# One store of a tree-masked attention kernel issued as two DMAs, of 60 and of 68 partitions

## The chip, the cores and the metric

The kernel runs on one core of one Trainium2 chip. The metric is the device time of one execution in microseconds (us). The inputs and outputs lie in the chip's memory (HBM), and the time includes loading the inputs and storing the result.

## The reference

Attention over 8 x 12 = 96 heads of 512 positions and 64 dimensions, in fp32. The mask is a binary tree: position i may look at itself and at its ancestors, (i-1)//2 and so on up to 0.

```
for i in range(seq):
    mask[i, i] = 1
    parent = i
    while parent > 0:
        parent = (parent - 1) // 2
        mask[i, parent] = 1
scores = einsum('bhqd,bhkd->bhqk', Q, K) * scale + (1 - mask) * (-1e9)
weights = softmax(scores)            # with the row's maximum taken off
out = einsum('bhqk,bhkd->bhqd', weights, V)
```

## The kernel before

A head's 512 rows lie on 128 partitions, four rows to a partition: a partition holds 4 x 64 fp32 values of one head, 1 KB in a row, both in HBM and in the output tile.

The 96 heads are worked in 48 pairs (`NP`), two heads at a time. Four heads are a quad (`NQ` = 24), and one output tile `of` holds a quad, so it is filled by two pairs: quad q by the pairs 2q and 2q + 1. There are 22 such tiles (`NOUT`), so that quads 22 and 23 take the tiles of quads 0 and 1 again.

The main loop (L644) goes over the pairs. For each it computes the scores on TensorE with the mask added as a code product, takes the exponent on ScalarE, multiplies by V and by a column of ones on TensorE (`values`), and divides on VectorE (`norm`, L495 and L496: a reciprocal and a product that writes `of`). Work on pair i - 1's values stands in the loop's step i. The order of the steps is written out by hand, and so are the queues.

GpSimd issues nearly all loads and stores. Its list (`pool_program`) has 21 stores of a whole quad (512 KB each, `store`, L503 and L504) in a fixed order with the loads and some copies; the last of them is that of quad 21. Five pieces of the output are not in this list:

- Quad 19 is stored by SyncE in the loop's step 41 (`store_apart`, L514 to L520), as two DMAs: the partitions 0 to 59 and 60 to 127 (`APART_ROWS` = 60).
- The pairs 44, 45 and 46 are stored by SyncE one at a time, in the loop's steps 45, 46 and 47 (L677 and L678), each by one DMA of 128 partitions and two heads, 256 KB. The heads of a pair are two apart in its quad.
- Of pair 47, SyncE stores one head and ScalarE the other (L680 and L681), 128 KB each.

A store waits for the product of `norm` that fills its part of `of`. SyncE has nothing else to do after the first loads: its instructions are issued in the order above, each when its wait is over. At the end the program waits until all stores have landed.

Of the kernel before, what the change touches and what calls it, by code (L numbers as in the profile page):

```python
# [98 lines left out]
def kernel(  # L99
# [7 lines left out]
    nc = tc.nc  # L107
    B, H, S, D = Q.shape
    P = nc.NUM_PARTITIONS
# [18 lines left out]
    Or = out.rearrange("b h (p t) d -> p (b h) (t d)", t=4)  # L128
# [71 lines left out]
    qTs, kTs, kqps, obs, ets, ofs = {}, {}, {}, {}, {}, {}  # L200
# [151 lines left out]
    def evac(i):  # L352
        if i >= WIDE:
            return evac_wide(i)
        kq = work.tile([P, 2, 16, 32], bf16, name="kq")
        kTs[i] = kq[:, 0, :, :]
        qTs[i] = kq[:, 1, :, :].rearrange("p (t u) c -> p t (u c)", t=4)
        src = kqps[i][:, :, 0:18, :]
        src = bass.AP(
            src.tensor, src.offset,  # L360
            [list(src.ap[0]), [1024, 2], [32, 8], [9 * 32, 2], [1, 32]],
        )
        nc.vector.tensor_copy(  # L363
            out=kq[:, :, :, :].rearrange("p k (x y) c -> p k x y c", y=2), in_=src
        )
# [4 lines left out]
    def scores1(i):  # L370

        sp = psS.tile([P, 2, 512], fp32, name="s1")
        for a in range(2):
            nc.tensor.matmul(  # L374
                out=sp[:, a, :], lhsT=k1code[64 * a:64 * a + CODE_ROWS, :],
                rhs=(q1code[64 * a:64 * a + CODE_ROWS, :] if i < WIDE
                     else q1wide[64 * a:64 * a + CODE_ROWS, :, :]),
                start=True, stop=False,
            )
        for a in range(2):  # L380
            nc.tensor.matmul(  # L381
                out=sp[:, a, :], lhsT=keys(i, a, TOP),
                rhs=qTs[i][64 * a:64 * a + 64, :, :].rearrange("p t c -> p (t c)"),
                start=False, stop=True,
            )
        et = etpool.tile([P, 2, 4, 128], bf16, name="e1")
        nc.scalar.activation(
            out=et[:, :, :, :].rearrange("p a t c -> p (a t c)"),
            in_=sp[:, :, :].rearrange("p a c -> p (a c)"),
            func=AF.Exp, scale=scale,  # L390
        ) if i < WIDE else nc.scalar.activation(  # L391
            out=et[:, :, :, :].rearrange("p a t (r u) -> p a (t r) u", u=2),
            in_=sp[:, :, :].rearrange("p a (u c) -> p a c u", u=2),
            func=AF.Exp, scale=scale,
        )
        ets[i] = et
# [31 lines left out]
    def scores2(i):  # L428
        if i >= WIDE:
            return scores2_wide(i)  # L430
        sp = psS.tile([P, 2, 4, 128], fp32, name="s2")
        flat = sp[:, :, :, :].rearrange("p a t c -> p a (t c)")
        for a in range(2):
            nc.tensor.matmul(
                out=sp[:, a, :, 32:128], lhsT=k2code[64 * a:64 * a + CODE_ROWS, :],
                rhs=q2code[64 * a:64 * a + CODE_ROWS, :].rearrange(
                    "p (t c) -> p t c", t=4
                )[:, :, 32:128],
                start=True, stop=False,
            )  # L440
        for t, lo, hi in ((2, 32, 192), (0, 192, 256), (3, 288, 448), (1, 448, 512)):
            for a in range(2):
                nc.tensor.matmul(
                    out=flat[:, a, lo:hi], lhsT=keys(i, a, TILE2[t]),
                    rhs=qTs[i][64 * a:64 * a + 64, :, :].rearrange("p t c -> p (t c)")[:, lo:hi],
                    start=False, stop=t == 1, skip_group_check=t in (2, 3),
                )
        nc.scalar.activation(
            out=e2s[i % NE][:, :, :, 32:128].rearrange("p a t c -> p (a t) c"),
            in_=sp[:, :, :, 32:128].rearrange("p a t c -> p (a t) c"),  # L450
            func=AF.Exp, scale=scale,
        )

    def values(i):

        if i < NP - 1:
            obs[i] = ob = psO.tile([P, 2, 512], fp32, name="ob")
        else:
            obs[i] = ob = psS.tile([P, 2, 512], fp32, name="s1")
        e1, e2, vt = ets[i], e2s[i % NE], vts[(head(i, 0) // VB) % NV]  # L460

        assert all(("vt", n, head(i, a)) in issued for n in range(10) for a in range(2))

        def product(e, a, t, tile_v, lo=0, hi=128, **flags):
            nc.tensor.matmul(  # L465
                out=ob[lo:hi, a, 65 * t:65 * t + 65],
                lhsT=e[:, a, PLACE[t], lo:hi],
                rhs=vt[:, head(i, a) % VB, tile_v, 0:D + 1],
                **flags,
            )  # L470

        def halves(a):
            for t in (0, 1):
                product(e2, a, t, 1 + SELF[t], 0, 64, start=False, stop=t == 1)
                product(e2, a, t, 1 + t, 64, 128, start=False, stop=t == 1)

        for a in range(2):
            for t in range(4):
                product(e1, a, t, 0, start=t == 0, stop=False)
            for t in (2, 3):  # L480
                product(e2, a, t, 1 + t, start=False, stop=False)
            if i == NP - 1:
                halves(a)
        if i < NP - 1:
            for a in range(2):
                halves(a)

    def norm(i):
        q, r = divmod(i, 2)
        if r == 0:  # L490
            ofs[q] = opool.tile([P, 4, 4, D], fp32, name="of")
        o4 = obs[i][:, :, 0:260].rearrange("p a (t c) -> p a t c", c=D + 1)
        rec = small.tile([P, 2, 4, 1], fp32, name="rec")
        for a, n in ((0, 2),) if i < NP - 1 else ((0, 1), (1, 1)):
            nc.vector.reciprocal(out=rec[:, a:a + n, :, :], in_=o4[:, a:a + n, :, D:D + 1])  # L495
            nc.vector.tensor_tensor(  # L496
                out=ofs[q][:, head(i, a) % 4:head(i, a + n - 1) % 4 + 1:head(i, 1) - head(i, 0), :, :],
                in0=o4[:, a:a + n, :, 0:D],
                in1=rec[:, a:a + n, :, :].to_broadcast([P, n, 4, D]),
                op=ALU.mult,  # L500
            )

    def store(eng, q, h0=0, n=4, step=1):  # L503
        return eng.dma_start(  # L504
            out=Or[:, 4 * q + h0:4 * q + h0 + step * (n - 1) + 1:step, :],
            in_=ofs[q][:, h0:h0 + step * (n - 1) + 1:step, :, :].rearrange(
                "p h t d -> p h (t d)"
            ),
        )


    APART, APART_AT, APART_ROWS = 19, 41, 60

    def store_apart():  # L514

        for p0, p1 in ((0, APART_ROWS), (APART_ROWS, P)):
            nc.sync.dma_start(
                out=Or[p0:p1, 4 * APART:4 * APART + 4, :],
                in_=ofs[APART][p0:p1, :, :, :].rearrange("p h t d -> p h (t d)"),
            )  # L520
# [123 lines left out]
    for i in range(NP + 1):  # L644
        steps = FIRST[i] if i < len(FIRST) else "SVT" if done < SIDE else "SVKQ"
        for step in steps:
            if step == "S" and i < NP:
                scores1(i)
                scores2(i)
            if step == "V" and i >= 1:  # L650
                values(i - 1)
                norm(i - 1)
                valued = True
            if step == "T" and done < NP:
                transpose(done)
                evac(done)
                done += 1
            if step == "K" and done < NP:
                transpose(done, (0,))
            if step == "Q" and done < NP:  # L660
                transpose(done, (1,))
                evac(done)
                done += 1
            if step == "X":
                spin("s1" if valued else "ob", 2)
            if step == "D":
                spread_by(nc.vector.tensor_copy, BY_VECTOR, STEADY_VECTOR, i)
            if step == "A":
                spread_by(nc.scalar.copy, BY_SCALAR, STEADY_SCALAR, i)
        if "D" not in steps:  # L670
            spread_by(nc.vector.tensor_copy, BY_VECTOR, STEADY_VECTOR, i)
        if "A" not in steps:
            spread_by(nc.scalar.copy, BY_SCALAR, STEADY_SCALAR, i)
        pool(i)
        if i == APART_AT:
            store_apart()
        if i >= NP - 3 and i < NP:  # L677
            store(nc.sync, (i - 1) // 2, (i - 1) % 2, 2, 2)  # L678
    assert not program
    store(nc.sync, NQ - 1, 1, 1)  # L680
    store(nc.scalar, NQ - 1, 3, 1)  # L681
# [30 lines left out]
```

## Time and profile before

| | |
|---|---|
| median of 3 runs | 136.35 us (135.78 to 136.41) |
| profiled execution, its own time | 136.35 us |
| its span, first to last instruction | 134.5 us |
| mean granted TensorE clock | 0.982 |
| busy: PE, VectorE, ScalarE, GpSimd | 116.7, 105.3, 110.9, 82.5 us |
| moved by DMA | HBM read 37.92 MB, written 12.58 MB |

The span runs from the first to the last instruction of the core; the execution's own time has 1.85 us around it. The profile gives start and length of each instruction, and for DMAs the issue on the issuing engine (SPq, ACTq and POOL are the queues of SyncE, ScalarE and GpSimd), the packets of each queue and the time from issue to landing. The queue called q0 carries GpSimd's transfers, q1 SyncE's and q10 ScalarE's. A DMA is carried out by up to 16 DMA engines side by side, each of which adds one to the transfer's semaphore when its part has landed. The trace records these increments.

### The profile page before, as it was taken

What the parts mean: (1) busy time and instruction counts of PE and PEld (TensorE: products, weight loads), DVE (VectorE), ACT (ScalarE), POOL (GpSimd) and SP (SyncE); (2) the same over time, 40 slices, a digit from 0 to 9 for tenths busy, and PEclk for the clock granted to TensorE, in tenths of its full rate; (3) what the DMA queues carried; (4) which work ended last, traced back from release to release, by engine and by line L of the source; (5) the groups of instructions that cost most, each with busy time, mean ns of one, the idle gap of its engine ahead of it and who ended that gap; (6) DMA issues with size and microseconds to landing.
All of it is one profiled execution on the core that took longest, in us unless ns stands there. A gap on an engine that the chain in (4) does not pass through costs nothing.

```text
span 134.5 us, 5483 instructions
## 1 busy us (share of the span) xinstructions
PE 116.7 (87%) x2385; PEld 79.7 (59%) x2385; DVE 105.3 (78%) x231; ACT 110.9 (82%) x169; POOL 82.5 (61%) x111
## 2 busy tenths in 40 slices
PE   6876989998797997799999899989899999999900
PEld 2342765665575665567576576757657676776600
DVE  2328699878969999987989979999598899666530
ACT  4359989989999899999999997979997797787800
POOL 6988636647465969899922279742999459512000
PEclk9999999999999999999999999999999999999975
DMA  4999999999999999999999999999999999999981
GB/s 126 215 168 193 202 192 197 199 200 196 201 199 204 198 198 196 208 198 201 198 205 197 310 251 204 289 271 240 323 212 329 229 293 400 403 398 405 374 319 44
DMA packets 37516, 32.23 MB, mean 240 GB/s; under 512 B 1357, under 2 KB 34765, under 8 KB 37493
## 3 DMA queue, kind: packets, MB, share of 16 engines
q0 software_dynamic: 35120, 29.63, 118.5%
q1 hardware_dynamic: 1813, 1.81, 4.0%
q10 hardware_dynamic: 560, 0.46, 1.1%
q8 instruction: 18, 0.29, 0.8%
q14 instruction: 5, 0.04, 0.1%
HBM read 37.92 MB, written 12.58 MB: 375 GB/s over the span
## 4 chain that ended last, share of the span: by engine, by line
PE 33%; ACT 23%; DVE 16%; DMA 15%; issue 7%; POOL 2%; ACTq 0%; POOLq 0%
PE ob L465 11%; DMA kst<-in_K_dram 10%; ACT vt L271 8%; ACT e L422 8%; DVE vt L271 6%; DMA vst<-in_V_dram 5%; DVE of L496 5%; PE s L374 4%; PE kqp L289 4%; ACT e L391 4%; PE s L406 4%; PE s L381 3%; PE kqp L319 3%; PE s L416 3%; DVE kq L347 2%
## 5 line engine op out<-in xcount | busy, mean ns | idle before, releaser
L391 ACT ACTIVATE e<-s 128x1024 bf16<-128x1024 f32 x40 | 40.9, 1023 | 8.8 <-PE s L381 7.9
L465 PE MATMUL ob<-vt,e 128*128 128x65 bf16 (+1 forms) x940 | 37.1, 197 | 3.0 <-DVE of L496 2.3
L465 PEld LDWEIGHTS <-e 128*128 128x128 bf16 (+1 forms) x960 | 30.3, 102 | 10.7 <-DVE of L496 2.2
L422 ACT ACTIVATE e<-s 128x384 bf16<-128x384 f32 x80 | 34.7, 489 | 0.0
L496 DVE TENSOR_TENSOR of<-ob,rec 128x512 f32<-128x512 f32 x47 | 32.5, 691 | 1.6
L271 DVE COPY vt<-vst 32x1024 bf16<-32x1024 bf16 (+8 forms) x56 | 29.9, 534 | 2.5 <-DMA vst<-in_V_dram 1.0
L271 ACT COPY vt<-vst 32x512 bf16<-32x512 bf16 (+5 forms) x30 | 23.4, 779 | 1.2 <-DMA vst<-in_V_dram 0.6
L504 POOL DMA_DIRECT2D out_dram<-of x21 | 16.2, 773 | 10.7 <-DVE of L496 3.4
L208 POOL DMA_DIRECT2D kst<-in_K_dram x19 | 16.0, 843 | 9.1 <-PE ob L465 2.9
L271 POOL COPY vt<-vst 32x256 bf16<-32x256 bf16 (+1 forms) x28 | 19.4, 693 | 2.7 <-DMA vst<-in_V_dram 1.6
L374 PE MATMUL s<-codes 40*128 40x512 bf16 x96 | 19.1, 393 | 1.8 <-ACT e L391 1.0
L495 DVE RECIPROCAL rec<-ob 128x8 f32<-128x8 f32 x47 | 9.6, 205 | 13.1 <-PE ob L465 12.2
L208 POOL DMA_DIRECT2D vst<-in_V_dram x17 | 14.1, 835 | 8.0 <-DMA vst<-in_V_dram 3.9
L289 PE MATMUL kqp<-ptile,kst 128*64 128x128 bf16 x320 | 16.6, 223 | 2.3 <-DVE kq L363 1.2
L381 PE MATMUL s<-kq 64*128 64x512 bf16 x96 | 18.4, 377 | 0.0
L343 DVE COPY kq<-kqp 128x512 bf16<-128x512 bf16 x40 | 16.6, 415 | 0.1
L416 PEld LDWEIGHTS <-kq 64*128 64x128 bf16 x320 | 12.3, 94 | 4.7
L406 PE MATMUL s<-codes 40*128 40x384 bf16 x80 | 13.7, 334 | 1.3
L416 PE MATMUL s<-kq 64*128 64x160 bf16 (+1 forms) x320 | 14.7, 208 | 0.0
L289 PEld LDWEIGHTS <-kst 128*64 128x64 bf16 x320 | 11.5, 111 | 4.8 <-issue 2.9
L223 POOL DMA_DIRECT2D qst<-in_Q_dram x13 | 9.6, 740 | 6.7 <-DMA vst<-in_V_dram 3.7
L347 DVE COPY kq<-kqp 128x1024 bf16<-128x1024 bf16 x20 | 13.6, 681 | 0.0
(37 smaller groups left out, 102.3 us busy)
## 6 DMA issues: line engine op xcount, KB each, us to landing
out_dram<-of POOLq DMA_DIRECT2D x21, 512.0 KB, 12.3
vst<-in_V_dram POOLq DMA_DIRECT2D x9, 512.0 KB, 12.3
kst<-in_K_dram POOLq DMA_DIRECT2D x8, 512.0 KB, 14.0
qst<-in_Q_dram POOLq DMA_DIRECT2D x7, 512.0 KB, 12.6
qst<-in_Q_dram POOLq DMA_DIRECT2D x8, 256.0 KB, 9.4
vst<-in_V_dram POOLq DMA_DIRECT2D x4, 256.0 KB, 8.7
kst<-in_K_dram POOLq DMA_DIRECT2D x4, 256.0 KB, 9.7
kst<-in_K_dram POOLq DMA_DIRECT2D x7, 128.0 KB, 9.2
```

The source lines that it names most:

```text
L208: return nc.gpsimd.dma_start(out=kept[b][:, h0 % size:h0 % size + n, :, :].rearrange("p h t d -> p h (t d)"), in_=src[:, h0:h0 + n, :],)
L271: return copy(out=dst, in_=src)
L289: nc.tensor.transpose(out=dst, in_=src, identity=perm)
L343: nc.vector.tensor_copy(out=kTs[i].rearrange("p (x y) c -> p x y c", y=2), in_=src)
L374: nc.tensor.matmul(out=sp[:, a, :], lhsT=k1code[64 * a:64 * a + CODE_ROWS, :], rhs=(q1code[64 * a:64 * a + CODE_ROWS, :] if i < WIDE else ...
L381: nc.tensor.matmul(out=sp[:, a, :], lhsT=keys(i, a, TOP), rhs=qTs[i][64 * a:64 * a + 64, :, :].rearrange("p t c -> p (t c)"), start=False, ...
L391: ) if i < WIDE else nc.scalar.activation(
L406: nc.tensor.matmul(out=flat[:, a, :, :].rearrange("p u (t c) -> p u t c", t=4)[:, :, :, 16:64], lhsT=k2code[64 * a:64 * a + CODE_ROWS, :], ...
L416: nc.tensor.matmul(out=flat[:, a, :, lo:hi], lhsT=keys(i, a, TILE2[t]), rhs=qT[64 * a:64 * a + 64, :, lo:hi], start=False, stop=t == 1, sk ...
L422: nc.scalar.activation(out=e2s[i % NE][:, a, :, 32:128].rearrange("p t (r u) -> p t r u", u=2), in_=flat[:, a, :, :].rearrange("p u (t r) ...
L465: nc.tensor.matmul(out=ob[lo:hi, a, 65 * t:65 * t + 65], lhsT=e[:, a, PLACE[t], lo:hi], rhs=vt[:, head(i, a) % VB, tile_v, 0:D + 1], **flags,)
L496: nc.vector.tensor_tensor(out=ofs[q][:, head(i, a) % 4:head(i, a + n - 1) % 4 + 1:head(i, 1) - head(i, 0), :, :], in0=o4[:, a:a + n, :, 0: ...
```

## The change

Pair 44's store becomes two DMAs on SyncE, of the partitions 0 to 59 and 60 to 127, with the same two heads. The stores of the pairs 45 and 46 go through the new helper too, as one DMA of 128 partitions each, with the access patterns that they had. Nothing is moved in the order of any other engine; SyncE has one more instruction. In the new file the helper shifts the line numbers: its DMA is L516, `store_apart`'s L524.

```
     APART, APART_AT, APART_ROWS = 19, 41, 60
+
+    def store_rows(i, p0, p1):
+        q, h0 = divmod(i, 2)
+        return nc.sync.dma_start(
+            out=Or[p0:p1, 4 * q + h0:4 * q + h0 + 3:2, :],
+            in_=ofs[q][p0:p1, h0:h0 + 3:2, :, :].rearrange("p h t d -> p h (t d)"),
+        )
 
     def store_apart():
...
         if i >= NP - 3 and i < NP:
-            store(nc.sync, (i - 1) // 2, (i - 1) % 2, 2, 2)
+            for p0, p1 in ((0, APART_ROWS), (APART_ROWS, P)) if i - 1 in (44,) else ((0, P),):
+                store_rows(i - 1, p0, p1)
     assert not program
```

## The prediction

> **What bounds the kernel now.** I read the windows of the last 25 us first, then SyncE's timeline, the DMA page and SyncE's waits. The columns of the windows are the length, each engine's busy time, the granted clock, the DMA engines' mean busy share and GB/s.
>
> ```profile
> 115.00:120.00 5.00, 5.00 (x107) 3.49 (x103) 3.11 (x7) 4.03 (x8) 1.93 (x3) 1.00 1.04 401
> 120.00:125.00 5.00, 5.00 (x104) 3.40 (x97) 3.31 (x8) 3.92 (x8) 0.75 (x1) 1.00 1.03 401
> 125.00:129.50 4.50, 2.63 (x54) 1.77 (x50) 2.72 (x8) 2.20 (x5) 0.00 (x0) 1.00 0.96 358
> 129.50:132.00 2.50, 0.00 (x0) 0.00 (x0) 0.00 (x0) 0.00 (x0) 0.00 (x0) 0.51 0.68 238
> 132.00:134.50 2.50, 0.00 (x0) 0.00 (x0) 0.00 (x0) 0.00 (x0) 0.00 (x0) 0.50 0.05 17
> ```
>
> Compute is over before 129.5. What follows is transfers alone, and they do not end together: 238 GB/s, then 17 GB/s. A last stretch at 17 GB/s is a few of the 16 DMA engines finishing after the rest have gone idle. SyncE's own issues (start, length), and VectorE's last product:
>
> ```profile
> 112.43 0.35 SPq L517 DMA_DIRECT2D out_dram<-of  x1
> 123.64 0.40 SPq L504 DMA_DIRECT2D out_dram<-of  x1
> 125.76 0.39 SPq L504 DMA_DIRECT2D out_dram<-of  x1
> 127.73 0.37 SPq L504 DMA_DIRECT2D out_dram<-of  x1
> 128.48 1.13 SPq L504 DMA_DIRECT2D out_dram<-of  x1
> 128.58 0.42 DVE L496 TENSOR_TENSOR of<-s,rec 128x256 f32<-128x256 f32 x1
> ```
>
> The 123.64 row is pair 44's store, the one that is cut in two. Then come pairs 45 and 46 and one head of pair 47. The DMA page (queue: packets, MB, share; issues: KB each, us to landing), and from SyncE's waits the one at the end:
>
> ```profile
> q1 hardware_dynamic: 1813, 1.81, 4.0%
> ...
> out_dram<-of SPq DMA_DIRECT2D x3, 256.0 KB, 6.1
> ...
> out_dram<-of SPq DMA_DIRECT2D x1, 272.0 KB
> ...
> out_dram<-of SPq DMA_DIRECT2D x1, 240.0 KB, 8.5
> out_dram<-of SPq DMA_DIRECT2D x1, 128.0 KB, 4.7
> out_dram<-of ACTq DMA_DIRECT2D x1, 128.0 KB, 3.8
> ```
>
> ```profile
> SPq L707 <- DMA out_dram<-of: 3.4, 2, 2.8
> ```
>
> The last SyncE store lands at 128.48 + 4.7 = 133.2 us and ScalarE's at 129.03 + 3.8 = 132.8. SyncE waits for them, and the span closes 1.3 us after the last landing. So the end is set by one DMA engine.
>
> **Which engine, and why.** The 272 KB row has no landing time. Quad 19 is already stored in 60 and 68 partitions, and this is its 68-row part. The packet count says why. SyncE's queue carries 40 packets of codes, 256 of first K, 512 of quad 19, 3 x 256 of pairs 44 to 46 and 128 of the last head: 1704. The other 109 of the 1813 are 4-byte semaphore writes, one for each DMA engine that a transfer uses: five transfers on 128 partitions make 5 x 16 = 80, the codes' 40 rows make 10, the 60 rows 15, and so the 68 rows make 4. In short, 60 rows go over 15 engines, 68 rows over only four, 17 rows each.
>
> The trace's landing records agree. The semaphore of the 68-row part has four late increments, at 129.34, 129.85, 130.06 and 130.55 us. Pair 44's last increment is at 131.21, pair 45's at 131.89, pair 46's at 132.54, ScalarE's at 132.88, SyncE's last at 133.22. Each step is one engine's share: 16 KB in 0.65 to 0.68 us, and 16 KB for the two single heads together. Only an engine that still owed 68-row packets until 130.55 can be 0.66 us behind it with pair 44. So the engine that ends the kernel, call it X, is one of the four that carry quad 19's 17 rows. From 130.55 it moves 64 packets of 1 KB in 2.67 us, 41.8 ns each. The last increments of the final store fall into groups: nine engines by 131.15, three at 131.70 to 131.93, three at 132.52 to 132.73, X at 133.22. Nine engines thus have 2.07 us of slack, X has none.
>
> **The change, part by part.**
> Removed: one DMA of 128 partitions, 16 KB on each of 16 engines. Added: 60 partitions, 4 rows x 2 KB = 8 KB on each of 15 engines, and 68 partitions, 17 rows x 2 KB = 34 KB on each of four. Bytes in all are the same. If the four are quad 19's four, and the 15 contain them, each of the four goes from 16 to 42 KB. The 16th engine loses 16 KB, the others 8 KB.
>
> Cost on X: 26 more packets of 1 KB behind the same earlier work. X's rate while GpSimd's stores also run on it is a round of one 4 KB packet and one 1 KB packet in 0.203 us (the spacing of the last GpSimd packets), 25.2 bytes per ns, so 26.6 thousand bytes cost at least 1.06 us. Alone, X takes 41.8 ns a packet by the landings and 42.3 by the spacing of its last packets: 1.09 to 1.10 us. I take 1.09, since X's GpSimd packets must be done by the time pair 44 moves in 0.66 us. The added semaphore write on X is already in the 41.8 ns, which is averaged over packets and their semaphore writes.
>
> Cost on SyncE: one more issue, 0.35 us by the 112.43 row, 1.13 us by the longest row. It starts at about 124.04 and the next store is ready only at 125.76, so 1.72 us of waiting covers either end. Behind it on SyncE are only stores; if the cover were gone, they would start up to 0.4 us later, which is still not on the path, because X owes earlier packets throughout.
>
> Cost for compute: nothing. GpSimd's last store is issued at 121.4, before the change, and no later tile takes the buffers of quads 22 or 23. VectorE, ScalarE and TensorE wait for no store in the rows after 123.64, so VectorE should still end near 129.0.
>
> Gain elsewhere: eleven engines lose 8 KB and one of them 16 KB, 0.33 to 0.66 us. They already end before X, so this is worth nothing.
>
> Sum: X lands at 133.22 + 1.09 = 134.31, the span becomes 134.5 + 1.09 = 135.6, and the profiled execution's 136.35 becomes 137.44. Its time equals the median of the runs (135.78 to 136.41), so no shift is needed. +1.09 us is +0.8%.
>
> The Trainium skill ("DMA: Bandwidth & Descriptors", section "Why a DMA increments its semaphore by 16 and not by 1") says that the engine count is the largest number up to 16 that divides the slowest dimension, and that SyncE's transfers take the lowest-numbered engines. The counts 15, 4 and 10 agree; that the four are always the same ones is shown by no row here, and by that rule the sum stands as above.
>
> **The rivals.**
> *Another four engines (not slower).* If the engines of a narrow transfer are dealt out in turn, the 34 KB miss X. X then only loses 8 KB, 0.33 us, and ends at 132.89. An early engine goes to at most 131.15 + 1.09 = 132.24. The time is 136.35 - 0.33 = 136.0, or 137.0 if the four include the engine that ends at 132.73. It decides as soon as X is outside the second four. Against it: quad 19's parts are the only ones on four engines, so nothing shows a second choice either way. Chance 0.06.
>
> *No concentration.* The change does not do what I read from the counts: the halves share all engines, and the time stays 136.35. The 109 semaphore writes and the four late landings speak against it. Chance 0.04. The same page of the Trainium skill ("Rules for kernel authors") says that two transfers to disjoint halves both spray over all 16 engines and are just not worth it. By that the time would not move; the 272 KB row disagrees for 68 partitions.
>
> *SyncE stalls behind the backlog (slower still).* The last issue took 1.13 us where the others take 0.4, though nothing else ran on SyncE: it may have met a full queue. With 26 more packets pending, later issues may be held longer. As long as X still has packets, this costs nothing on X. It counts if SyncE is held until an earlier store has landed. A store needs about 1.55 us from issue to its first landing (ScalarE: 129.03 to 130.58), plus 0.33 us for its 8 KB. Held until pair 45 has landed on X (131.89 + 1.09 = 132.98), the last head would land at 134.86: 138.0 us. Held until pair 46 (133.63): 135.51, 138.6 us. The 123.64 and 125.76 rows, unheld with quad 19's backlog on X, speak against it. Chance 0.07.
>
> **How the numbers follow.** The forecast, the same four engines, has 0.83, and the time is its own: 137.4. Its own spread is the price's 1.06 to 1.10 plus the runs' 0.6 us, 136.9 to 137.9. The range goes down to 136.8, which takes in the mixed case of the other four, and up to 138.3, which takes in half of the stall. About 0.5%, 0.68 us, can be told from no change. Slower by more: 0.78 of the forecast and the stall's 0.07, 0.85. Within: 0.05 of the forecast, 0.04 of the other four, 0.03 of no concentration, 0.12. Faster: 0.02 and 0.01, 0.03.
>
> **What would show it.** SyncE's queue has 1816 packets (1813 - 16 + 15 + 4), and a 136 KB issue without a landing time stands beside a 120 KB one. VectorE still ends near 129.0. The last SyncE store takes 5.8 us to land instead of 4.7, ScalarE's 4.9 instead of 3.8. The window after 132 us moves more than 17 GB/s. Semaphore increments of pairs 45 and 46 on four engines come about 1.1 us later, on the others 0.3 us earlier. Wrong: if the last landing is unmoved or earlier, the four engines are not X's; if a SyncE issue of pair 45, 46 or 47 is longer than 2 us and X has a gap, the stall is real; if VectorE's end moves, I missed a wait.

## The result, and the profile after

| | before | changed |
|---|---|---|
| median of 22 runs each | 136.22 us | 137.47 us |
| ratio, 95% interval | | 1.0087 (1.0067 to 1.0108) |
| profiled execution: span | 134.5 us | 135.8 us |
| last landing of quad 19's 68 rows | 130.55 us | 130.23 us |
| last landing of all | 133.22 us | 134.64 us |
| VectorE's last product ends | 129.00 us | 130.83 us |

The change costs 0.87% of 136.22 us, 1.19 us (0.91 to 1.47). The forecast was 1.09 us. The ratio leaves out the slow executions (138.69 us before, 139.18 and 139.54 us changed), so it is not exactly that of the medians.

The windows of the changed kernel (length, busy time of each engine, granted clock, DMA share, GB/s):

```profile
120.00:125.00 5.00, 5.00 (x99) 3.35 (x97) 3.42 (x9) 3.92 (x8) 0.75 (x1) 1.00 1.01 389
125.00:129.50 4.50, 4.35 (x88) 2.99 (x84) 2.54 (x6) 3.85 (x7) 0.00 (x0) 1.00 0.79 293
129.50:132.00 2.50, 0.10 (x4) 0.00 (x0) 1.16 (x5) 0.00 (x0) 0.00 (x0) 1.00 0.92 297
132.00:134.50 2.50, 0.00 (x0) 0.00 (x0) 0.00 (x0) 0.00 (x0) 0.00 (x0) 0.53 0.30 103
```

After 132 us there is still a stretch with a few DMA engines at work, now at 103 GB/s where it was 17. Compute, on the other hand, also ends later: TensorE is busy for 4.35 us of the window that starts at 125, where it was busy for 2.63. The changed kernel's SyncE issues show when that delay came in:

```profile
113.77 0.36 SPq L524 DMA_DIRECT2D out_dram<-of  x1
114.17 0.38 SPq L524 DMA_DIRECT2D out_dram<-of  x1
125.48 0.33 SPq L516 DMA_DIRECT2D out_dram<-of  x1
125.85 1.28 SPq L516 DMA_DIRECT2D out_dram<-of  x1
127.60 1.17 SPq L516 DMA_DIRECT2D out_dram<-of  x1
129.57 0.39 SPq L516 DMA_DIRECT2D out_dram<-of  x1
130.31 0.48 SPq L504 DMA_DIRECT2D out_dram<-of  x1
```

Quad 19's store is issued at 113.77 against 112.43, before SyncE meets anything that was changed. So 1.34 of the 1.83 us were there by then. Pair 44's first part is the first instruction that the change touches, and it waits for VectorE's product: it is issued at 125.48 against 123.64, 1.84 us later. So the whole delay was there before the first changed instruction ran. Whether this later compute has a part in the 1.19 us is taken up below. The DMA page of the changed kernel:

```profile
q1 hardware_dynamic: 1816, 1.81, 4.1%
...
out_dram<-of SPq DMA_DIRECT2D x2, 256.0 KB, 5.0
...
out_dram<-of SPq DMA_DIRECT2D x1, 272.0 KB
...
out_dram<-of SPq DMA_DIRECT2D x1, 136.0 KB
out_dram<-of SPq DMA_DIRECT2D x1, 128.0 KB, 4.1
out_dram<-of ACTq DMA_DIRECT2D x1, 128.0 KB
out_dram<-of SPq DMA_DIRECT2D x1, 120.0 KB, 5.6
```

1816 packets are the 1813 of before less 16 semaphore writes, and 15 and 4 in their place. The 136 KB part has no landing time, as quad 19's 272 KB part had none. Its semaphore has four late increments, at 131.72, 131.90, 131.97 and 132.58 us. Pair 45's last four follow at 132.41, 132.58, 132.64 and 133.27, each 0.67 to 0.69 us behind: one engine's 16 KB. (ScalarE's row lacks a landing time for another reason: in this kernel its store shares a semaphore with the load of the codes.)

### The profile page after: what moved, and what is told of

Same layout as the page of the kernel before. It is cut to its first block, busy times and chain, and to the rows that moved or that the text cites. A ratio compares the mean times of both kernels' runs of the same rounds, so it can differ in the third digit from the quotient of the medians.

```text
span 135.8 us, 5484 instructions
## 1 busy us (share of the span) xinstructions
PE 117.0 (86%) x2385; PEld 79.6 (59%) x2385; DVE 106.8 (79%) x231; ACT 110.8 (82%) x169; POOL 83.1 (61%) x111
## 3 DMA queue, kind: packets, MB, share of 16 engines
q1 hardware_dynamic: 1816, 1.81, 4.1%
## 4 chain that ended last, share of the span: by engine, by line
PE 36%; DVE 24%; ACT 18%; DMA 7%; POOL 6%; issue 5%; ACTq 0%; POOLq 0%
PE ob L465 12%; DVE vt L271 8%; DMA vst<-in_V_dram 7%; DVE of L496 7%; ACT e L422 6%; ACT e L391 5%; ACT vt L271 5%; PE s L374 5%; PE kqp L289 5%; PE s L406 4%; PE s L381 3%; PE kqp L319 3%; DVE kq L347 3%; PE s L416 3%; DVE kq L343 3%
## 5 line engine op out<-in xcount | busy, mean ns | idle before, releaser
L271 DVE COPY vt<-vst 32x1024 bf16<-32x1024 bf16 (+8 forms) x56 | 31.7, 566 | 3.3 <-DMA vst<-in_V_dram 1.9
```

The lines of the kernel that those rows point to most:

```text
L271: return copy(out=dst, in_=src)
```

## The experiments

Theory A, that of the prediction: the kernel ends when the most loaded of a few DMA engines has moved its bytes, and pair 44's 68 rows put 26 KB more on each of the four engines that already carry quad 19's. Theory B: the second DMA costs by itself, or holds SyncE. Theory C: the later compute is the cause. Ratios are to the kernel before, with 95% intervals.

**Two DMAs, but of 64 partitions each.** It keeps the second DMA and takes the concentration away.

```
-for p0, p1 in ((0, APART_ROWS), (APART_ROWS, P)) if i - 1 in (44,) else ...
+for p0, p1 in ((0, 64), (64, P)) if i - 1 in (44,) else ((0, P),):
```

> Pair 44's store as two DMAs again, but of 64 and 64 partitions. 64 rows go over 16 engines, so each engine gets 8 KB twice, the 16 KB it had before. Theory (bytes on quad 19's four DMA engines): no change, 136.2 us, ratio 1.000 within 0.003; the queue of SyncE then has 1813 + 16 = 1829 packets. Rival (the second DMA itself costs: SyncE's issue, its wait behind the backlog, or completion): it stays as slow as with 60 and 68, 137.4 us, ratio 1.009.

Measured: 1.0005 (0.9983 to 1.0027), 1829 packets. A second DMA by itself costs nothing that can be told; B as the cause of the 1.19 us is out. The Trainium skill's rule that two halves spray over the same 16 engines ("DMA: Bandwidth & Descriptors", "Rules for kernel authors") holds for two halves of 64, as the 1829 packets show. 60 and 68 are not halves, and the 1816 packets of the changed kernel show 15 and four engines.

**Pairs 44 and 45 both as 60 and 68.**

```
-... if i - 1 in (44,) else ...
+... if i - 1 in (44, 45) else ...
```

> Pairs 44 and 45 both stored as 60 and 68 partitions. Theory: 26 more packets on the four engines, another 26 x 41.8 ns = 1.09 us, so 136.2 + 2.18 = 138.4 us, ratio 1.016; SyncE's last store takes about 7 us to land. Rival (SyncE held by the backlog): more than twice the one step, 139 us or more, with a SyncE issue of pair 46 or 47 held for over 2 us and a gap on the late engines. Rival (nothing more to lose after the first): 137.4.

Measured: 1.0217 (1.0179 to 1.0254), 2.95 us on the 135.94 of the runs of before beside it. That is more than A's 2.18. In its profile, which is of the slowest of its six executions (139.65 us), the DMA engines stand half idle from 129.5 to 132 us, with a busy share of 0.49, while stores wait (windows, then SyncE's issues):

```profile
125.00:129.50 4.50, 4.29 (x86) 2.91 (x83) 2.44 (x7) 3.69 (x7) 0.00 (x0) 1.00 0.76 276
129.50:132.00 2.50, 0.00 (x0) 0.00 (x0) 1.10 (x4) 0.00 (x0) 0.00 (x0) 1.00 0.49 92
```

```profile
125.69 1.76 SPq L516 DMA_DIRECT2D out_dram<-of  x1
127.56 2.11 SPq L516 DMA_DIRECT2D out_dram<-of  x1
129.71 0.33 SPq L516 DMA_DIRECT2D out_dram<-of  x1
130.14 0.40 SPq L516 DMA_DIRECT2D out_dram<-of  x1
130.64 2.06 SPq L504 DMA_DIRECT2D out_dram<-of  x1
```

Three of its issues last about 2 us. So a held SyncE, as in the prediction's third rival, is seen here beside the bytes. The records of the packets show a second thing: 0.49 of 16 engines is about eight at work, and 92 GB/s is little for eight, when a share of 1.03 went with 401 GB/s in the kernel before. From 130 to 133 us 109 of SyncE's 1 KB packets took over 80 ns each, up to 333 ns, where in the kernel before every 1 KB packet behind quad 19's part took 46 ns at most. Which of the two brings the other, and how much of the surplus each makes, is not shown.

**Quad 19 whole, and quad 19 whole with pair 44 split.** These turn the prior load around.

```
 def store_apart():
-    for p0, p1 in ((0, APART_ROWS), (APART_ROWS, P)):
+    for p0, p1 in ((0, P),):
```

> The kernel before, with quad 19 stored by SyncE as one DMA of 128 partitions. Each engine then gets 32 KB of it: quad 19's four engines lose 84 - 32 = 52 KB (2.2 us), eleven gain 16 KB (0.67 us), the sixteenth gains 32 KB (1.3 us). Theory: the four end at 133.22 - 2.17 = 131.05 and are no longer last; the late three of the other engines end at 132.73 + 0.67 = 133.4, or 134.1 if the latest is the sixteenth. Time 136.2 + 0.2 to 0.8 = 136.4 to 137.0 us. Rival (the end is not set by the four engines' bytes): no change, 136.2, or the end moves with compute.

> Quad 19 whole as in the run before this one, and pair 44 as 60 and 68 partitions. Theory: the four end at 131.05 + 1.09 = 132.1, still not last, and the others lose 8 KB (the sixteenth 16 KB), so the same change that costs 1.09 us beside a split quad 19 here brings 0.33 to 0.66 us against the run with quad 19 whole: 135.9 to 136.6 us. Rival (the second DMA itself costs): 1.1 us more than with quad 19 whole, 137.5 to 138.1 us.

Measured: quad 19 whole 136.47 us, ratio 1.0057 (1.0035 to 1.0078); with pair 44 as 60 and 68 beside it 136.13 us, 1.0021 (1.0005 to 1.0037). The same edit that costs 1.19 us beside a split quad 19 goes the other way here, by 0.0036 of 135.94, 0.49 us (0.34 by the medians); the two intervals just overlap, so the size of this gain is known roughly. The last landings are 133.71 and 133.14 us. In the second run pair 44's 68 rows land at 129.95 at the latest. With 48 KB still to come, 2.0 us at 41.8 ns per KB, the four engines would end at about 132.0, an estimate, and are no longer the last. The DMA page of that run:

```profile
out_dram<-of SPq DMA_DIRECT2D x1, 512.0 KB, 12.3
out_dram<-of SPq DMA_DIRECT2D x2, 256.0 KB, 4.1
...
out_dram<-of SPq DMA_DIRECT2D x1, 136.0 KB
out_dram<-of SPq DMA_DIRECT2D x1, 128.0 KB, 3.0
```

The 136 KB part is on four engines here too (no landing time), but the last head lands 3.0 us after its issue, where it took 3.7 us with quad 19 whole and no pair split.

**Other rows, another pair.** With quad 19 split, pair 44 as 119 and 9 partitions, or pair 46 as 60 and 68.

```
+... ((0, 119), (119, P)) if i - 1 in (44,) ...      # the one
+... if i - 1 in (46,) ...                           # the other
```

> Quad 19 split as before, and pair 44 stored as 119 and 9 partitions. By the rule seen in the packet counts 119 rows go over seven engines (17 rows, 34 KB each) and 9 rows over nine (1 row, 2 KB each). Theory, with the engines counted from the same first one each time: seven engines, quad 19's four among them, go from 16 to 36 KB, 20 more packets, 20 x 41.8 ns = 0.84 us, so 135.9 + 0.84 = 136.8 us, ratio 1.006; SyncE's queue has 1813 packets (16 - 7 - 9 = 0 difference). Rival (the engines of a narrow transfer are dealt out in turn): the four may be missed and lose 14 KB, 0.6 us, ratio below 1.000. Rival (the second DMA itself costs): ratio 1.009 as with 60 and 68.

> Quad 19 split as before, pair 46 instead of pair 44 stored as 60 and 68 partitions. Theory (only the bytes on the four engines count, and they owe packets to the end anyway): the same 26 packets, 1.09 us, 137.0 us, ratio 1.008. Rival (SyncE held): the 68 rows now stand directly ahead of the last head's store, which starts later; if its late landing sets the end, 137.5 us or more, ratio 1.012 or more, and SyncE's last issue takes over 2 us.

Measured: 119 and 9 give 1.0123 (1.008 to 1.0166), 1813 packets; pair 46 gives 1.0096 (1.0062 to 1.0129). Pair 46 agrees with A: no difference can be told between splitting pair 44 and pair 46. With 119 rows the engine counts 7 and 9 agree with the packets, and the sign says that the seven engines take in the one that ends last, which speaks against their being dealt out in turn. But the size is off: 1.67 us (1.09 to 2.26) where the bytes give 0.84.

**Two improvements tried.** Quad 19 whole, and two late pairs cut so that the late engines lose bytes.

```
+... if i - 1 in (44, 45) ...                                       # the one
+{44: ((0, 119), (119, P)), 45: ((0, 120), (120, P))}.get(i - 1, ...)  # the other
```

> Quad 19 whole, pairs 44 and 45 both as 60 and 68 partitions. With quad 19 whole and pair 44 split, the last landings were 133.14 and 132.89 us on two engines and 132.05 or less on the other fourteen. Theory: the second split takes 16 KB (0.67 us) from the engine outside the 15 and 8 KB (0.33 us) from the other late one, to 132.5 and 132.6; the four gain 1.09 us, from at most 132.0 to at most 133.1. Time 135.6 to 136.1 us, ratio 0.997 to 1.002. Rival (SyncE held by two narrow DMAs, as in the run with both pairs split beside a split quad 19): early engines idle while stores are ready, 0.8 us more, ratio 1.005 or more.

> Quad 19 whole, pair 44 as 119 and 9 partitions (seven engines with 34 KB, nine with 2 KB), pair 45 as 120 and 8 (fifteen engines with 16 KB, eight with 2 KB). Against quad 19 whole with pair 44 as 60 and 68: the sixteenth engine loses another 16 KB (132.5 if it was the one at 133.14), an engine from the eighth to the fifteenth loses 6 to 8 KB (132.6 if it was the one at 132.89), seven engines get 36 + 18 KB. Theory: the end is 132.6 to 133.0, time 135.6 to 136.0 us, ratio 0.997 to 1.001. Rival (four DMAs in place of two hold SyncE): ratio 1.005 or more.

Measured: 0.9992 (0.9964 to 1.002) and 1.0012 (0.9983 to 1.0041). Neither can be told from the kernel before, so no version here beats it.

**The 68 rows issued last.** To see whether the surplus of the run with both pairs split is SyncE's hold: its two 68-row parts are issued behind pair 47's head. And the changed kernel was profiled once more, for theory C.

```
+store_rows(i - 1, 0, APART_ROWS if i - 1 in (44, 45) else P)
...
 store(nc.sync, NQ - 1, 1, 1)
+for p in (44, 45):
+    store_rows(p, APART_ROWS, P)
```

> Quad 19 split as before, pairs 44 and 45 as 60 and 68 partitions, but the two 68-row parts are issued by SyncE last of all, behind pair 47's head. Bytes on each engine are those of the run with both pairs split (ratio 1.0217 there, where the bytes alone give 1.016). Theory (bytes on the four engines, and there a surplus from SyncE being held ahead of pair 45's and 46's stores): the hold has nothing behind it now, so 26 + 26 packets remain, 2.18 us, ratio 1.016. Rival (the surplus is the price of narrow DMAs themselves): ratio 1.021 again.

> The changed kernel once more, for a second profile of it. Theory: from the last landing of quad 19's 68-row part to the last landing of all, the latest engine moves 90 KB where it moved 64 before: 90 x 41.8 ns = 3.76 us against 2.67, whenever compute ends; VectorE's end may lie anywhere between 128.9 and 130.9 us as it did in the other profiles. Rival (the time came from a later compute, 1.8 us in the first profile of it): the span follows VectorE's end, and with an end near 129.0 it would be 134.5 again.

Measured: 1.0163 (1.0132 to 1.0194), the 1.016 of the bytes. SyncE's longest issue in the tail is 0.47 us. The intervals of 1.0163 and 1.0217 overlap, and the slow packets became fewer along with the hold (19 over 80 ns behind quad 19's part, where it was 119), so the hold as the cause of that surplus is possible, not shown.

The second profile of the changed kernel had VectorE's end at 130.67, late again, and a span of 135.5 us. The test with an early end did not come about. Its latest engine needed 4.91 us from quad 19's last landing (129.38) to the end (134.29), not 3.76: the expectation failed. GpSimd's last store, in that profile, landed at 130.40, 1.0 us after quad 19's part, where in the profile of before the two ended together (130.52 and 130.55). So in that profile quad 19's part need not mark the point from which SyncE's packets have the engine alone.

**119 rows last, and 119 rows in place again.**

```
+store_rows(i - 1, 119 if i - 1 in (44,) else 0, P)
...
+store_rows(44, 0, 119)      # behind pair 47's head
```

> Quad 19 split as before, pair 44 as 119 and 9 partitions, but the 119 rows are issued by SyncE last of all. The bytes on each engine are those of the run with 119 and 9 in place, which measured ratio 1.0123 where the bytes alone give 1.006. Theory (bytes, and a surplus from SyncE being held 2.3 and 2.2 us ahead of pair 45's and 46's stores): nothing stands behind the long part now, so 20 packets remain, 0.84 us, ratio 1.006, and SyncE's issues of pairs 45 and 46 take 0.4 us. Rival (119 rows on seven engines cost more than their bytes): ratio 1.012 again.

> The kernel with pair 44 as 119 and 9 partitions in place once more, beside the one with the 119 rows last, on the same chip. Theory: a surplus over the bytes' 1.006, near the 1.012 measured, with SyncE's issues held by more than 1 us. Rival (the first measurement was off): 1.006 as with the 119 rows last.

Measured: 1.0123 (1.0084 to 1.0163) with the 119 rows last, 1.011 (1.0059 to 1.0161) in place. With the 119 rows last SyncE is not held (0.40 us at most in the tail), and the time is no better. So the hold doesn't explain the surplus of the 119 rows; what does is open. In the profile with the 119 rows last the bytes alone account for the tail: 129.79 to 133.30 us, 3.51 us for 84 KB. That profile was of the fastest of its executions (136.27 us of 136.27 to 138.31), so of this kernel the surplus lies in executions of which no trace was taken. The first profile of the 119 rows in place (137.48 us) has a tail near the bytes too, 3.60 us, but quad 19's part lands at 130.90 in it, 0.35 us later than in the profile of before. As one execution of each, that is a hint and no more.

The two profiles of the 119 rows in place are the clearest evidence on theory C. They are of one and the same kernel, and VectorE's last product starts 1.53 us apart in them:

```profile
128.84 0.42 DVE L496 TENSOR_TENSOR of<-s,rec 128x256 f32<-128x256 f32 x1
```

```profile
130.37 0.42 DVE L496 TENSOR_TENSOR of<-s,rec 128x256 f32<-128x256 f32 x1
```

Their spans are 135.7 and 135.6 us. So the late compute comes and goes with the execution, and between these two it did not move the end: the loaded engines are behind either way. Nor does it come with the new code: in the five profiles with 64 and 64, pair 46, both pairs with the 68 rows last, the 119 rows in place (the first) and the 119 rows last, compute ended between 128.7 and 129.4. The run with quad 19 whole and pair 44 split says the same from the other side: compute ended at 130.32 there, 1.3 us later than before, and the span was 134.4.

## Why the prediction was right

**Engine counts: right.** 1816, 1829 and 1813 packets came out as 15 and 4, 16 and 16, and 7 and 9 engines say.

**The same four engines: right.** If the four had missed the engine that ends last, the time would have fallen by 0.33 us, or risen by some 0.6 with the other late engine of the prediction among them. It rose by 1.19 (0.91 to 1.47), and pair 45's last four increments sit one 16 KB step behind pair 44's. One step of the reading was too strong: "only" an engine with 68-row packets until 130.55 could end last. GpSimd's last store landed at 130.52, so an engine that carried that would have fitted the landings as well. The runs settle it: a cost of 1.19 us says that the latest engine is one of pair 44's four, and as the same edit costs nothing with quad 19 whole, it was quad 19's 68 rows that had made this engine the last.

**26 packets at 41.8 ns: right in size for 26 KB, and in part by luck.** 1.09 us against 1.19 (0.91 to 1.47), and pair 46 1.3 us (0.8 to 1.8). All profiles with quad 19 split can be asked for the price: how long it took from the last landing of quad 19's part to the end of all, and how many KB the latest engine then still owed.

| | GpSimd's last landing, against quad 19's | KB left on the latest engine | measured | at 41.8 ns per KB |
|---|---|---|---|---|
| before | -0.03 us | 64 | 2.67 us | 2.67 us |
| 64 and 64 | -0.41 us | 64 | 2.67 us | 2.67 us |
| 119 rows last | -0.30 us | 84 | 3.51 us | 3.51 us |
| 119 rows in place | -0.49 us | 84 | 3.60 us | 3.51 us |
| pair 46 split | +0.52 us | 90 | 3.79 us | 3.76 us |
| changed | +0.47 us | 90 | 4.41 us | 3.76 us |
| changed, again | +1.02 us | 90 | 4.91 us | 3.76 us |
| 119 rows in place, again | +0.70 us | 84 | 4.29 us | 3.51 us |
| both pairs, 68 rows last | +0.25 us | 116 | 5.44 us | 4.85 us |
| both pairs | +1.03 us | 116 | 7.14 us | 4.85 us |

The price itself was read off the first row. Where GpSimd's stores are done first, it holds within 0.1 us. Where they are not, five of six profiles take 0.6 to 2.3 us longer, those of the changed kernel among them. GpSimd's packets left over can explain a part of that, if they ran on the latest engine, which the records do not say; the slow packets told above are another part. So no profile shows the 90 KB of the changed kernel at the bare price. Over all executions the sum of the bytes fits the changed kernel, pair 46 and both pairs with the 68 rows last; it was too small for the 119 rows (0.84 against 1.67 us) and for both pairs in place (2.18 against 2.95). That bytes on the engines that are already last set the direction is shown. What adds to them in some kernels and not in others is open, and as long as it is, a forecast within 0.1 us is in part luck.

**SyncE's cost: nothing, as said, but bounded too low.** The longest issue was expected at 1.13 us; the 68-row part took 1.28, and up to 2.3 us were seen elsewhere. It ended at 127.13, before the next store began at 127.60. The run with 64 and 64 is the harder test. The second half's issue, the first row, held SyncE for 2 us, and pair 45's product was done at 126.14, before that issue ended:

```profile
124.80 2.01 SPq L516 DMA_DIRECT2D out_dram<-of  x1
126.93 1.16 SPq L516 DMA_DIRECT2D out_dram<-of  x1
```

So pair 45's store, the second row, was issued 0.79 us late, and the time did not move. That bears out the prediction's argument that later stores are not on the path while the latest engine owes earlier packets. The rival of a held SyncE was right to have a chance: holds are seen with one split pair, where they do not decide, and with two, where their part in the surplus is open.

**Compute near 129.0: wrong as a number.** It ended at 130.83 and 130.67. I had taken one profile's end for a constant of the kernel. By the prediction's own sign a moved end means a missed wait; the 1.84 us that were there before the first changed instruction speak against it. For the same reason the landing times were off: the last SyncE store took 4.1 us to land, not 5.8, since it was issued 1.83 us later into the same backlog. The other engines' increments could not come 0.3 us earlier either: pair 45's first is at 130.87, where it was at 127.77. The last landing itself moved by 1.42 us in the profile.

**The gain elsewhere: nothing, as said,** while the four are last. Quad 19 whole is the state in which it counts.

## What to carry to other kernels

When transfers end a kernel, ask which DMA engine ends last and how many bytes it still owes; the packet count and the landing increments tell both. In these runs a store's partition count decided on how many engines it ran (128 and 64 rows on 16, 60 on 15, 119 on seven, 68 on four), so cutting 128 rows into 60 and 68 is not a neutral cut: it moves bytes onto a few engines, and whether that helps or hurts depends on what these already carry. The same edit cost 1.19 us beside an earlier narrow store and gained some 0.3 to 0.5 us without it.

## What was not expected of the hardware

An issue on SyncE that lasts 0.3 to 0.5 us by itself lasted 0.9 to 2.3 us in most of the kernels with quad 19 split, and never over 0.42 us in the four with quad 19 whole. What holds it was not found; it was absent with quad 19 split too when the long parts were issued last. In the run with both pairs split SyncE's 1 KB packets, 46 ns in the tail of before, took up to 333 ns. And compute ended 1.53 us apart in two executions of one kernel, with spans 0.1 us apart.
